# A hybrid decoder layer on one core: the memory tokens' projection one column tile later

## The chip, the cores and the metric

The kernel runs on one core of one Trainium2 chip. The time is device time in microseconds (us) of one execution, the median of several; lower is better. The engines are PE (matrix products), ACT, DVE and POOL (elementwise work of different kinds) and SP, which here only issues transfers; POOL issues the gathers from the paged cache. Matrix operands lie in SBUF, products in PSUM.

## The reference

One layer of a decoder trunk runs for two groups that share the weights: a prompt of 2048 tokens and a sample group of 8 x 4 tokens. The core of it:

```
h = rms_norm(x, pre_g)
z = h @ w_in                                   # 1024 -> 11 x 512 columns
ca, cb, cg, pu, pg, q, k, v, sg, mq, mg = split(z)
y_c = conv_branch(ca, cb, ...)                 # gated causal convolution, width 31
y_p = pool_branch(pu, ...)                     # causal means of 2, 4, 8, 16 tokens
y_s = stick_breaking_attention(q, k, v)        # prompt: causal; sample: 8192 cached tokens each
mk, mv = split(rms_norm(mem, mem_g) @ w_mem_kv)  # 256 memory tokens, 2 x 512 columns
y_m = softmax_attention(mq, mk, mv)
mix = concat(y_c*silu(cg), y_p*silu(pg), y_s*silu(sg), y_m*silu(mg))
y = rms_norm(x + rms_norm(mix @ w_out, post_g), final_g)
```

The new keys and values, the last rows of the convolution and pooling inputs and the memory keys and values are outputs too.

## The kernel before

**Stages.** First the projection z, with the sample group's attention over its cache woven into it; then the prompt's attention (`sb_prompt`), with small leftovers of the sample group as side work; then the output product. What PE does is in the order in which the program is written. A scheduler places the instructions of the other engines and of the queues, within what the data allow.

**The projection.** Each operand is split into a high and a low half, and a product is three matmuls (high by high, high by low, low by high) for each of the 8 slices of 128 of the 1024 inputs, so 24 matmuls (`mm3`). The prompt goes in two parts of 1024 tokens; part 0 also holds the 32 sample rows. A column tile is 128 columns of `w_in`: (q, 0) is the first of q. Part 0 has 44 column tiles, each in three row tiles of 384, 384 and 288 rows, part 1 has 44 in two row tiles of 512. `GROUPS[part]` lists them in the order in which they are done; most groups hold one column tile, the first of part 0 holds (q, 0) and (q, 1) together, then come (q, 2), (q, 3), (k, 0) to (k, 3), (v, 0) to (v, 3) and the rest. `z_groups` runs groups: it opens each, multiplies row tile by row tile, empties the product (`z_evac`) and yields the cost of every half product.

**Weights.** `SEQ_W` is the order in which weight tiles are loaded by SP (`load_w`, tile wr, 512 KB) and split (`split_w`: ACT makes whi, POOL wlo). There are two pairs of whi and wlo and two raw tiles; `fill_w` refills them whenever a column tile is done. The eight column tiles of the memory tokens' weight (`"mem"`) are inserted into this list by a table of pairs (number, place).

**The start.** `x_first` loads, normalises and transposes the prompt's first 1024 rows while the first group runs on what is ready. Once 768 rows are done, `mem_norm` is added to the tasks; it does the same for the 256 memory tokens (tiles xtm, xpsm, mhi, mlo). `tasks.step()` gives every live task one step. Then `mem_tokens` is handed to `z_groups` as `between`: after each product of a row tile one memory product (mz, 24 matmuls of 256 columns) is made, eight in all, and `mem_rows` empties it (mzt), turns it back and stores it (mko, mvo, and for later use mkd, mvd).

**The sample group.** When the memory pool is closed, `main` runs all remaining groups. Each cost it yields adds to `due`; whenever `due` reaches 1, one step of the generator `sample` is taken. It gathers cached keys and values (kt, vt, by POOL), turns the keys on DVE (T), forms scores (sSA), weights and products with the values (sO), in 64 rounds of about four steps. The line numbers are those of the profile:

```
total = 39 * 1056 / 512 * 5.12 + 44 * 1024 / 512 * 5.12
rate = (4 * NPAGE + 8) / (SEND * total)        # NPAGE 64, SEND 0.97
```

When the generator ends, its pool is closed, and the loader of the prompt's attention is made on the same space (`sb_loader`); it issues the first block's loads at once: four of kT, four of Q, one of V. These and the stores of the projection's last results (gsd, gcd, mixd, and ydw for the convolution) go through SP's one queue in order. `sb_prompt` then works in blocks of 512 queries, (head pair, block): scores S, two sigmoids on ACT (gam, be), a scan on DVE (E), products on POOL, transposes (AT) and products with the values (av).

Of the kernel before, what the change touches and what calls it, by code (L numbers as in the profile page):

```python
# [86 lines left out]
def kernel(  # L87
# [66 lines left out]
    def z_tile(name):  # L154
        return zps.tile([P, 512], F32, tag="z", name=name)
# [80 lines left out]
    def mm3(ps, whi, wlo, xhi, xlo, c0, c1):  # L236

        n = ND * 3
        i = 0
        for d in range(ND):  # L240
            for w, x in ((whi, xhi), (whi, xlo), (wlo, xhi)):
                pe.matmul(ps[:, : c1 - c0], lhsT=w[:, d, :], rhs=x[:, d, c0:c1], start=i == 0, stop=i == n - 1)
                i += 1
                if i == n // 2:
                    yield
# [12 lines left out]
    def k4(name, shape, dt):  # L258
        return st.tile(shape, dt, tag="k4", name=name, bufs=K4)
# [62 lines left out]
    def x_stream(part, ahead, tile_):  # L322

        todo = [(xp[PART * part + P * t : PART * part + P * (t + 1), :], P, P * t, f"p{part}_{t}") for t in range(8)]
        ready = []
        gpre = None
        loaded = []

        def norm():
            n, xt = loaded.pop(0)  # L330
            ready.append(norm_rows(xt, todo[n][1], gpre, rs1[:, n : n + 1]))

        for i, (src, rows, col, nm) in enumerate(todo):
            while len(ready) + len(loaded) < min(len(todo), i + ahead):
                n = len(ready) + len(loaded)
                xt = tile_(f"xt{todo[n][3]}")
                sp.dma_start(xt[: todo[n][1]], todo[n][0])
                if gpre is None:
                    gpre = big(f"gpre{part}")[:, :D]
                    sp.dma_start(gpre, pre_g[0].partition_broadcast(P))  # L340
                loaded.append((n, xt))
            if i == 0:
                yield
                yield
                norm()
            if loaded:
                norm()
            while X["free"] < col + rows:
                yield
            for hf in range(2):  # L350
                split_rows(ready[i], rows, xhi, xlo, col, hf, nm)
                if hf:
                    X["done", part] = col + rows
                yield
# [24 lines left out]
    def mem_norm(mp, M):  # L379
        mg_bc = mp.tile([P, D], F32, name="mg_bc", bufs=1)  # L380
        sp.dma_start(mg_bc, mem_g[0].partition_broadcast(P))
        M["hi"] = mp.tile([P, ND, NMEM], F32R, name="mhi", bufs=1)
        M["lo"] = mp.tile([P, ND, NMEM], F32R, name="mlo", bufs=1)
        rows = []
        for t in range(2):
            xt = mp.tile([P, D], F32, tag="xt", name=f"xtm{t}", bufs=XB)
            sp.dma_start(xt, mem_prompt[0, P * t : P * (t + 1), :])
            rows.append(norm_rows(xt, P, mg_bc))
        yield
        yield  # L390
        for t in range(2):
            for hf in range(2):
                split_rows(rows[t], P, M["hi"], M["lo"], P * t, hf, f"m{t}")
                yield
# [260 lines left out]
    def z_open(part, kind, c):  # L655

        s = {}
        if kind == "ca":
            U = s["U"] = state["U"] = big(f"U{part}_{c}")
            pool.tensor_copy(U[:, 0:CH], uhist[:, c, :])  # L660
        elif kind == "pu":
            s["pf"] = big(f"pf{part}_{c}")
            pool.tensor_copy(s["pf"][:, 0:PH], phist[:, c, :])
        elif kind == "mg":
            state["g"] = big(f"g{kind}{part}_{c}")
        elif kind == "pg":
            s["plw"] = st.tile([P, P], F32, tag="plw", name=f"plw{part}_{c}", bufs=1)
            wq.dma_start(s["plw"], pool_w[0, c])
        elif kind == "mq":
            s["kv"] = mem_kv(c, part)  # L670
        return s
# [80 lines left out]
    def z_close(part, kind, c, s):  # L752
        if kind == "cb":
            U = state["U"]
            pool.tensor_copy(uhist[:, c, :], U[:, PART : PART + CH])
            tasks.add(conv_dw(c, U, part))
        elif kind == "pu":
            pool.tensor_copy(phist[:, c, :], s["pf"][:, PART : PART + PH])
            state["d"] = pool_group(c, s["pf"], part)

    MAIN = ("ca", "cb", "pu", "cg", "pg", "mg")
    GROUPS = {0: [[("q", 0), ("q", 1)]] + [[(k, c)] for k in ("q", "k", "v") for c in range(2 if k == "q" else 0, 4)],
              1: [[(k, c)] for k in ("k", "v", "q") for c in range(4)]}
# [3 lines left out]
        GROUPS[part] += ([] if part == 0 else [[("ca", 3)], [("cb", 3)]]) + [[("pu", 3)], [("mg", 3)], [("mq", 3), ("pg", 3)]]  # L767
        GROUPS[part] += ([[("ca", 3)], [("cb", 3)]] if part == 0 else []) + [[("cg", 3), ("sg", 3)]]
    SEQ_W = [(p_,) + it for p_ in range(2) for g in GROUPS[p_] for it in g]
    for i, at in ((0, 3), (1, 4), (2, 5), (3, 7), (4, 8), (5, 9), (6, 11), (7, 12)):  # L770
        SEQ_W.insert(at, (0, "mem", i))
    raw, wsplit = {}, {}

# [5 lines left out]
    def fill_w(n=2):  # L779

        while len(wsplit) < n and (raw or SEQ_W):
            if not raw:
                next_raw()
            it = next(iter(raw))
            wsplit[it] = split_w(raw.pop(it), "%d%s%d" % it)
        while n == 2 and len(raw) < WR and SEQ_W:
            next_raw()

    def z_groups(part, groups, between=None):

        for g in groups:
            last = part == 0 and g is GROUPS[0][-1]
            fill_w()
            if last:
                X["free"] = 0
                tasks.add(x_stream(1, XA, lambda n: k4(n, [P, D], F32)))
            opened = [z_open(part, kind, c) for kind, c in g]
            cols = COLS[part]
            for ti, (c0, c1) in enumerate(cols):
                for j, (kind, c) in enumerate(g):  # L800
                    while X["done", part] < c1:
                        yield 0.0
                    ps = z_tile(f"z{part}{kind}{c}_{ti}")
                    half = 2.56 * (c1 - c0) / 512
                    for _ in mm3(ps, *wsplit[(part, kind, c)], xhi, xlo, c0, c1):
                        yield half
                    z_evac(part, kind, c, ti, c0, c1, ps, opened[j])
                    if ti == len(cols) - 1:
                        z_close(part, kind, c, opened[j])
                        del wsplit[(part, kind, c)]  # L810
                        fill_w()
                    if last and j == 1:
                        X["free"] = c1
                    yield half
                    if between is not None:
                        next(between, None)
                        yield 0.0
# [962 lines left out]
    with tc.tile_pool(name="mem", bufs=2, side="right") as mp:  # L1780
        M = {}
        xst = x_first(lambda n: mp.tile([P, D], F32, tag="xt", name=n, bufs=XB))
        for _ in range(X0):
            next(xst)
        tasks.add(xst)
        for _ in z_groups(0, GROUPS[0][:1]):
            tasks.step()
            if X["done", 0] >= XM and not M:
                M["gen"] = mem_norm(mp, M)
                tasks.add(M["gen"])  # L1790
        for _ in M["gen"]:
            pass

        sp.dma_start(conv_sample[0][:, 0 : CH - TS, :], state_conv[0][:, TS:CH, :])
        sp.dma_start(pool_sample[0][:, 0 : PH - TS, :], state_pool[0][:, TS:PH, :])
        sp.dma_start(bias_bc, sb_bias[0].partition_broadcast(P))
        dve.tensor_scalar(out=nbias_bc, in0=bias_bc, scalar1=-1.0, scalar2=None, op0=ALU.mult)
        tasks.add(params_and_histories(mp))
        mem = mem_tokens(mp, M)
        for _ in z_groups(0, GROUPS[0][1:4], mem):  # L1800
            tasks.step()
        for _ in range(3):
            tasks.step()
# [9 lines left out]
    sample = sample_all()  # L1813

    def main():
        yield from z_groups(0, GROUPS[0][4:12])
        tasks.add(later_stats())
        yield from z_groups(0, GROUPS[0][12:14])
        tasks.add(sample_keys())
        yield from z_groups(0, GROUPS[0][14:])  # L1820
        tasks.add(state_rows(0))
        yield from z_groups(1, GROUPS[1][:-2])
        tasks.add(state_rows(1))
        yield from z_groups(1, GROUPS[1][-2:])
# [205 lines left out]
    for n, x in enumerate(parts):  # L2030
# [8 lines left out]
        prod, i, h = x  # L2039
# [55 lines left out]
```

## Time and profile before

| what | value |
|---|---|
| median of three runs | 2423.75 us (2419.15 to 2426.24) |
| the profiled execution: its time / its span | 2418.47 us / 2416.7 us |
| mean granted clock of PE | 0.982 |
| PE busy | 2285.6 us |
| DVE / POOL / ACT busy | 1718.3 / 1306.8 / 1117.5 us |
| moved by the transfer engines | 562.14 MB, mean 233 GB/s |

Rows of a time line give the start, the length, the engine, the line, the operation, output and inputs and the count; in brackets stands how long the engine was idle just before and what ended that. Numbers of buffers are left out of names in the trace. PEld is PE's loading of weights, which overlaps its products; SPq is SP's transfer queue, whose rows are issues and not the transfers themselves.

### The profile page before, as it was taken

To read this page: it belongs to the slowest core of one execution; us is meant where nothing else is said; L and a number is where in the kernel's file an instruction comes from. 1 tells how busy PE (TensorE), PEld (TensorE's weight loads), DVE (VectorE), ACT (ScalarE), POOL (GpSimd) and SP (SyncE) were. 2 spreads that over 40 slices of the span, in tenths; PEclk is the share of its full clock that TensorE was granted. 3 is DMA by queue.
4 is the path that set the end of the run, shared out by engine and by line. 5 is a ranking of instruction groups with operands and counts; after the bars stand their busy time and mean duration, and the time that the engine had idled before them with its cause. 6 is when DMAs were issued, how large, how long until landed. Compare 5 with 4: busy or idle time off the path is not lost. (4 is left out here: it accounts for less than half of the span.)

```text
span 2416.7 us, 42137 instructions
## 1 busy us (share of the span) xinstructions
PE 2285.6 (95%) x15962; PEld 1774.5 (73%) x15962; DVE 1718.3 (71%) x2410; ACT 1117.5 (46%) x1939; POOL 1306.8 (54%) x1333
## 2 busy tenths in 40 slices
PE   7999999999999999999999998899999998989897
PEld 6998978898888777777777776455555556768775
DVE  5333774959757664587877777879798846687998
ACT  5322343242442322124242434788989954443554
POOL 2554544556574555655556564667877755453430
PEclk9999999999999999999999999999999999999998
DMA  5789988887778899987887767834333227887764
GB/s 179 223 260 298 348 290 287 284 272 263 263 254 292 277 344 325 323 287 262 275 270 269 262 218 179 239 79 117 89 88 79 64 64 242 266 272 254 245 234 170
DMA packets 340437, 562.14 MB, mean 233 GB/s; under 512 B 28481, under 2 KB 212929, under 8 KB 323834
## 3 DMA queue, kind: packets, MB, share of 16 engines
q1 hardware_dynamic: 284858, 290.72, 39.2%
q0 software_dynamic: 55376, 268.72, 31.3%
q8 instruction: 126, 2.06, 0.3%
q14 instruction: 77, 0.63, 0.1%
HBM read 469.28 MB, written 90.68 MB: 232 GB/s over the span
## 5 line engine op out<-in xcount | busy, mean ns | idle before, releaser
L959 DVE STREAM_TRANSPOSE T<-kt 128x1024 f32<-128x1024 f32 x256 | 308.9, 1226 | 183.4 <-PE sSA L972 177.2
L926 POOL DMA_INDIRECT vt<-in_cache_v_dram,idv x256 | 251.6, 983 | 242.1 <-PE sO L1011 181.5
L617 DVE SCALAR_TENSOR_TENSOR cacc<-U,par,cacc 128x512 f32<-128x512 f32 x480 | 360.2, 750 | 11.8
L1311 POOL TENSOR_TENSOR be<-be,E 128x512 f32<-128x512 f32 (+2 forms) x320 | 303.8, 957 | 118.4 <-DVE E L1302 52.4
L1302 DVE TENSOR_TENSOR_SCAN E<-gam,cr,ZM 128x513 f32<-128x513 f32 x192 | 232.8, 1262 | 15.1 <-ACT gam L1287 14.2
L926 POOL DMA_INDIRECT kt<-in_cache_k_dram,idk x128 | 126.2, 986 | 201.9 <-DVE T L959 146.8
L1322 PEld LDWEIGHTS AT<-ident,be 128*128 128x128 f32 x1088 | 117.7, 142 | 127.6 <-ACT at L1328 45.4
L1287 ACT ACTIVATE gam<-S,nbias_bc 128x1024 f32<-128x1024 f32 (+1 forms) x160 | 172.6, 1079 | 50.8 <-ACT be L1289 18.9
L1915 PE MATMUL acc<-wohi,mh 128*128 128x512 f32 (+1 forms) x480 | 193.3, 403 | 0.6 <-ACT mh L1669 0.6
L1915 PE MATMUL acc<-wolo,mh 128*128 128x512 f32 (+1 forms) x480 | 189.6, 395 | 0.0
L1915 PE MATMUL acc<-wohi,ml 128*128 128x512 f32 x448 | 178.1, 398 | 11.6 <-DVE ml L1680 11.6
L1282 PE MATMUL S<-kT,Q 128*128 128x512 f32 (+1 forms) x640 | 177.9, 401 | 6.8 <-DMA Q<-qd 2.7
L1289 ACT ACTIVATE be<-S,bias_bc 128x1024 f32<-128x1024 f32 (+1 forms) x160 | 171.6, 1073 | 0.0
L1322 PE MATMUL AT<-ident,be 128*128 128x128 f32 x1088 | 158.1, 284 | 14.1 <-ACT at L1328 4.2
L1338 PE MATMUL av<-at,V 128*64 128x512 f32 (+3 forms) x640 | 153.0, 557 | 1.7 <-DVE sbo L1343 1.7
L972 PE MATMUL sSA<-T,W 128*32 128x128 f32 x4096 | 139.2, 277 | 6.4 <-DVE T L959 5.6
L972 PEld LDWEIGHTS sSA<-T,W 128*32 128x32 f32 x4096 | 104.7, 110 | 43.6 <-issue 35.3
L1680 DVE TENSOR_TENSOR ml<-mr,mh 128x512 fp32r<-128x512 f32 x108 | 98.1, 914 | 38.4 <-ACT mh L1669 38.2
L1282 PEld LDWEIGHTS S<-kT,Q 128*128 128x128 f32 x640 | 107.1, 195 | 23.0 <-ACT be L1289 3.5
L1011 PE MATMUL sO<-vt,saT 128*32 128x512 f32 x1024 | 122.4, 592 | 0.0
L1299 DVE TENSOR_TENSOR_SCAN E<-gam,ZM 128x128 f32<-128x128 f32 (+3 forms) x128 | 96.4, 802 | 30.1 <-ACT gam L1287 25.2
L1328 ACT COPY at<-AT 128x512 f32<-128x512 f32 x192 | 108.9, 655 | 14.4 <-PE AT L1322 14.4
(571 smaller groups left out, 6043.7 us busy)
## 6 DMA issues: line engine op xcount, KB each, us to landing
Q<-qd SPq DMA_DIRECT2D x64, 256.0 KB
mr<-mixd SPq DMA_DIRECT2D x32, 512.0 KB
mr<-mixd SPq DMA_DIRECT2D x48, 256.0 KB
wor<-in_w_out_dram SPq DMA_DIRECT2D x20, 512.0 KB
xtp<-in_x_prompt_dram SPq DMA_DIRECT2D x16, 512.0 KB
kT<-kd SPq DMA_DIRECT2D x64, 128.0 KB
wor<-in_w_out_dram SPq DMA_DIRECT2D x32, 256.0 KB
msd<-mr SPq DMA_DIRECT2D x32, 256.0 KB
```

What stands on the lines that cost most here:

```text
L617: dve.scalar_tensor_tensor(out=ps, in0=U[:, a + k : a + k + H], scalar=wd[:, k : k + 1], in1=ps, op0=ALU.mult, op1=ALU.add)
L926: pool.indirect_dma_start(out=dst, out_offset=None, in_=rows, in_offset=bass.IndirectOffsetOnAxis(ap=idx, axis=0))
L959: dve.transpose(T[:, 2 * hh : 2 * hh + 2].rearrange("p s j t -> p (s j t)"), kt[:, 2 * hh : 2 * hh + 2].rearrange("p s j d -> p (s j d)"))
L972: pe.matmul(sSs[n][32 * g : 32 * g + 32, P * ml : P * (ml + 1)], lhsT=W[:, jj, :], rhs=T[:, :, jj, :], start=i == 0, stop=i == 3, tile_pos ...
L1282: pe.matmul(S[:, j, :w], lhsT=Q[hh][:, x, P * (q2 + j) : P * (q2 + j + 1)], rhs=KT[hp, hh, kc][:, :w], start=x == 0, stop=x == 1)
L1287: act.activation(out=ga[:, :, 512 - w : 512], in_=S[:, :, :w], func=AF.Sigmoid, bias=nbias_bc[:, h : h + 1], scale=-1.0)
L1289: act.activation(out=be[:, :, :w], in_=S[:, :, :w], func=AF.Sigmoid, bias=bias_bc[:, h : h + 1])
L1302: dve.tensor_tensor_scan(out=E[:, j][:, ::-1], data0=ga[:, j][:, ::-1], data1=ZM[:, 0:1].to_broadcast([P, 513]), initial=carry[hh, q2][:, ...
L1311: pool.tensor_tensor(out=be[:, j, :m], in0=be[:, j, :m], in1=E[:, j, 513 - w : 513 - w + m], op=ALU.mult)
L1322: pe.transpose(ap_[:, P * qt : P * (qt + 1)], A[hp, qb, kc, hh, qt][:, P * r : P * (r + 1)], ident)
L1338: pe.matmul(av[64 * hh : 64 * hh + 64, c], lhsT=V[:, 4 * kc + r, 64 * hh : 64 * hh + 64], rhs=ats.pop((hp, qb, kc, r, hh))[:, c], start=dg ...
L1915: pe.matmul(o[:rows], lhsT=m[a][:, k, :rows], rhs=W[prod, 4 * h + k][w], start=not cont and h == k == n == 0, stop=h == 1 and k == 3 and n ...
```

## The change

Three things move by one group in part 0. The table puts the eight memory weights one place later into `SEQ_W`. The start now runs two groups, (q, 0) with (q, 1), and (q, 2), before the memory products are handed over. The memory products go between the row tiles of (q, 3), (k, 0) and (k, 1) instead of (q, 2), (q, 3) and (k, 0), and `main` begins with (k, 2) instead of (k, 1). The line with `total` is unchanged, and nothing else is.

```
-    for i, at in ((0, 3), (1, 4), (2, 5), (3, 7), (4, 8), (5, 9), (6, 11), (7, 12)):
+    for i, at in ((0, 4), (1, 5), (2, 6), (3, 8), (4, 9), (5, 10), (6, 12), (7, 13)):
         SEQ_W.insert(at, (0, "mem", i))
...
-        for _ in z_groups(0, GROUPS[0][:1]):
+        for _ in z_groups(0, GROUPS[0][:2]):
             tasks.step()
             if X["done", 0] >= XM and not M:
                 M["gen"] = mem_norm(mp, M)
...
         mem = mem_tokens(mp, M)
-        for _ in z_groups(0, GROUPS[0][1:4], mem):
+        for _ in z_groups(0, GROUPS[0][2:5], mem):
             tasks.step()
...
     def main():
-        yield from z_groups(0, GROUPS[0][4:12])
+        yield from z_groups(0, GROUPS[0][5:12])
         tasks.add(later_stats())
```

More of the change, by code (lines that the diff above doesn't have):

```diff
@@ L769 @@
     SEQ_W = [(p_,) + it for p_ in range(2) for g in GROUPS[p_] for it in g]
-    for i, at in ((0, 3), (1, 4), (2, 5), (3, 7), (4, 8), (5, 9), (6, 11), (7, 12)):
+    for i, at in ((0, 4), (1, 5), (2, 6), (3, 8), (4, 9), (5, 10), (6, 12), (7, 13)):
         SEQ_W.insert(at, (0, "mem", i))
@@ L1785 @@
         tasks.add(xst)
-        for _ in z_groups(0, GROUPS[0][:1]):
+        for _ in z_groups(0, GROUPS[0][:2]):
             tasks.step()
@@ L1799 @@
         mem = mem_tokens(mp, M)
-        for _ in z_groups(0, GROUPS[0][1:4], mem):
+        for _ in z_groups(0, GROUPS[0][2:5], mem):
             tasks.step()
@@ L1815, in main @@
     def main():
-        yield from z_groups(0, GROUPS[0][4:12])
+        yield from z_groups(0, GROUPS[0][5:12])
         tasks.add(later_stats())
```

## The prediction

> **What bounds the kernel now.** I read the page first, then busy time by stretches of 50 us, then the time lines of PE (the matmul engine) and of SP's transfer queue where PE idles. A row of a stretch shows its length, busy us and count of PE, its weight loads, DVE, ACT and POOL, then granted clock, transfer share and GB/s.
>
> ```profile
> span 2416.7 us, 42137 instructions
> PE 2285.6 (95%) x15962; PEld 1774.5 (73%) x15962; DVE 1718.3 (71%) x2410; ACT 1117.5 (46%) x1939; POOL 1306.8 (54%) x1333
> 50.00:100.00 50.00, 48.45 (x353) 47.09 (x353) 19.80 (x36) 16.32 (x29) 25.94 (x19) 1.00 0.59 184
> 100.00:150.00 50.00, 46.79 (x310) 45.17 (x310) 18.08 (x43) 14.17 (x28) 28.00 (x31) 0.97 0.79 242
> 350.00:400.00 50.00, 45.32 (x399) 40.78 (x398) 24.04 (x38) 25.37 (x46) 24.60 (x23) 0.93 0.74 253
> 1450.00:1500.00 50.00, 44.55 (x212) 33.98 (x211) 40.29 (x60) 23.13 (x37) 20.63 (x38) 0.98 0.63 170
> 1500.00:1550.00 50.00, 43.11 (x252) 25.59 (x251) 37.50 (x55) 34.80 (x43) 27.97 (x41) 0.85 0.90 264
> ```
>
> PE is busy 95% of the span, in an order that is written out by hand. An edit that only reorders is therefore paid, or earns, where PE idles. The memory products lie in the first two stretches: 4.8 us idle in 100 us, nothing large. The largest hole is at 1490 us, where the projection with the sample group's work woven in ends and prompt attention begins: 5.5 and 6.9 us idle, at a lower granted clock.
>
> ```profile
> 1472.76 1.96 PE L1011 MATMUL sO<-vt,saT 128*32 128x512 f32 x16
> 1490.28 0.40 PE L242 MATMUL z1sg<-xhi,wlo1sg 128*128 128x512 f32 x1
> 1492.15 1.65 PE L1282 MATMUL S<-kT,Q 128*128 128x256 f32 x8 [1.47 <-DVE sg1sg L714]
> 1499.71 2.90 PE L1282 MATMUL S<-kT,Q 128*128 128x256 f32 x8 [1.68 <-DMA Q<-qd]
> 1503.67 1.19 PE L1282 MATMUL S<-kT,Q 128*128 128x256 f32 x4 [1.05 <-DMA Q<-qd]
> 1513.79 0.64 PE L1165 MATMUL smS<-mkbT,qm 128*32 128x256 f32 x8 [2.08 <-DMA mkbT<-mkTd]
> ```
>
> In the brackets stands the idle time just before and what ended it: three times a transfer. The sample's last products (sO, 1472.76) are 17.5 us ahead of the projection's last (1490.28); that lead is what the change touches.
>
> **The change part by part.** *The memory products.* Eight products of 24 matmuls and their weights go from the groups q2, q3, k0 to q3, k0, k1. Nothing is added or removed. ACT, which makes the high halves of the weights (whi) and empties the products (zt, mzt), before:
>
> ```order
> L232 COPY whi0mem_605<-wr0mem_250 128x1024
> L688 ACTIVATE zt0q_2_597<-z0q_2_572 128x288
> L688 ACTIVATE zt0q_0_648<-z0q_0_614 128x384
> L232 COPY whi0mem_680<-wr0mem_570 128x1024
> L416 COPY mzt_685<-mz_654 128x256
> ```
>
> And in the changed kernel, from the same place on:
>
> ```order
> L232 COPY whi0q_605<-wr0q_250 128x1024
> L688 ACTIVATE zt0q_2_597<-z0q_2_572 128x288
> L688 ACTIVATE zt0q_0_635<-z0q_0_610 128x384
> L688 ACTIVATE zt0q_1_666<-z0q_1_641 128x384
> L232 COPY whi0mem_705<-wr0mem_570 128x1024
> ```
>
> q3's weights are split where the first memory weights were, and q2's tiles follow each other without a memory product (mz) between. SP and POOL shift alike: one weight load of 512 KB stands for another, and one low half for another. What that can cost is a weight that comes late. The tightest case of before is k0's weight, split only once q3 is done:
>
> ```profile
> 100.83 2.40 POOL L233 TENSOR_TENSOR wlo0k<-wr0k,whi0k 128x1024 fp32r<-128x1024 f32 x1 [0.93 <-ACT whi0k L232]
> 103.28 0.45 PE L242 MATMUL z0k<-xhi,wlo0k 128*128 128x384 f32 x1 [0.20 <-POOL wlo0k L233]
> ```
>
> That cost 0.2 us. The same step comes once more in the new order, from q2 to the first memory weight, with the 24 matmuls of q3's first tile to cover it. I take 0; the ends are the 1.7 us that the stretch from 100 idles beyond the one from 50, either way. The rows of the tokens themselves stay: PE, DVE and POOL's order is unchanged up to q1's last tile, with the transposes of the memory rows in it.
>
> *The sample group's start.* `main` begins one group later. Its steps are dealt out by `due`, at 264 / (0.97 x 862.4) = 0.3156 per unit of projection cost, and `total` still counts 39 column tiles in part 0 where `main` now has 38. The sample's generator needs 268 calls, which are due at 268 / 0.3156 = 849.2 units. `main` had 862.4 units, a lead of 13.2; now it has 851.8, a lead of 2.6, one half of the last product. So sO and all that hangs on it move from 17.5 us to 12 matmuls ahead of the projection's end. Through the rest of the projection the sample's work lies 10.6 units later against the same tiles; PE's sum is the same, the chance meetings are others. I cost that at 0 with wide ends (rivals).
>
> *The first loads of prompt attention.* They are issued when the sample ends, and go on SP's queue. Before, with the semaphores that each waits for:
>
> ```order
> L601 DMA mixd<-po_3_1_14477 128x4x128 [waits DMAHW4_49,DVE_49]
> L1238 DMA kT_0_0_14518<-kd 64x512 [waits DMAHW5_49,PE_49]
> L1239 DMA Q_0_0_14519<-qd 64x2x512 [waits DMASW5_49,DMASW7_49,DMASW3_49,DMAHW6_49,DMASW1_49,PE_49]
> L1238 DMA kT_0_0_14518<-kd 64x512 [waits DMAHW7_49]
> L1239 DMA Q_0_0_14519<-qd 64x2x512 [waits DMAHW0_49]
> ```
>
> And in the changed kernel:
>
> ```order
> L540 DMA mixd<-mo_3_512_14567 128x4x128 [waits DMAHW7_49,DVE_49]
> L624 DMA ydw<-acc_3_1_14646 128x512 [waits DMAHW0_49,Activation_49]
> L1238 DMA kT_0_0_14601<-kd 64x512 [waits DMAHW1_49,PE_49]
> L1239 DMA Q_0_0_14602<-qd 64x2x512 [waits DMASW5_49,DMASW7_49,DMASW3_49,DMAHW2_49,DMASW1_49,PE_49]
> L1238 DMA kT_0_0_14601<-kd 64x512 [waits DMAHW3_49]
> ```
>
> The nine loads of block (0,0) (kT, Q and V) have moved behind four stores, the last of them the end of the convolution, `ydw<-acc_3_1`. When these rows ran before:
>
> ```profile
> kT<-kd SPq DMA_DIRECT2D x12, 128.0 KB
> Q<-qd SPq DMA_DIRECT2D x12, 256.0 KB
> V<-vd SPq DMA_DIRECT2D x1, 1024.0 KB
> 1474.78 0.53 SPq L1238 DMA_DIRECT2D kT<-kd  x1
> 1480.05 0.54 SPq L1244 DMA_DIRECT2D V<-vd  x1
> 1480.68 4.57 SPq L716 DMA_DIRECT2D gsd<-sg1sg  x1
> 1490.30 0.32 SPq L624 DMA_DIRECT2D ydw<-acc  x1
> 1490.67 0.46 SPq L1238 DMA_DIRECT2D kT<-kd  x1
> 1492.49 0.53 SPq L1239 DMA_DIRECT2D Q<-qd  x1
> 1504.94 7.97 SPq L1158 DMA_DIRECT2D mkbT<-mkTd  x8
> 1479.00:1482.00 3.00, 3.00 (x15) 2.42 (x14) 2.93 (x5) 0.00 (x0) 0.00 (x0) 1.00 0.97 219
> 1482.00:1485.00 3.00, 3.00 (x15) 2.42 (x14) 2.89 (x4) 0.60 (x1) 0.00 (x0) 1.00 1.09 203
> 1485.00:1488.00 3.00, 3.00 (x15) 2.42 (x14) 2.86 (x5) 0.00 (x0) 0.00 (x0) 1.00 1.21 289
> 1488.00:1491.00 3.00, 2.68 (x12) 1.83 (x10) 1.58 (x3) 0.81 (x2) 0.49 (x2) 1.00 0.79 265
> 1491.00:1494.00 3.00, 1.65 (x8) 1.14 (x8) 0.69 (x1) 1.38 (x3) 1.43 (x7) 1.00 0.69 223
> 1494.00:1497.00 3.00, 0.90 (x5) 0.70 (x6) 2.19 (x4) 3.00 (x5) 1.15 (x3) 1.00 0.72 145
> 1500.00:1503.00 3.00, 2.61 (x8) 1.70 (x7) 2.40 (x4) 1.80 (x4) 2.39 (x5) 0.50 1.07 223
> ```
>
> They ran from 1474.78 under a PE that was full. Now they start at about 1490.6, and block (1,·)'s loads, on which the scores at 1499.71 and 1503.67 already wait, come behind them. By issue alone: nine issues are 5.8 us (1474.78 to 1480.6), less 1.8 that the queue stood anyway between kT and Q (1490.67 to 1492.49): 4.0 us, the low end. By volume: four times 128 KB and 256 KB and V's 1 MB are 2.62 MB; at the mean of the three stretches from 1479 (237 GB/s) 11.1 us, of which 2.4 fit into the unused transfer share of 1488 to 1497 (3 us times 0.21, 0.31, 0.28): 8.7 us. The high end is 5.8 + 4.6 = 10.4, if the store behind V stands as long again (row 1480.68). I take 8.0, near the volume, because the transfer share is full from 1500 on, and a little under it since three stores that ran behind these loads now go ahead of them. The cover, 16 us of projection, is gone; what is late next is block (1,·), then the mkbT loads of 1504.94 and the smS at 1513.79, which stands in PE's order and holds all behind it. Nothing later in the attention stage waits for a fixed time, so the delay stays to the end.
>
> The Trainium skill (DMA: Bandwidth & Descriptors, section Bandwidth) gives 341 GB/s for a 1 MB transfer; by that figure, an estimate, the volume would take 7.7 us and the term would be 5.3. The rows above, with runs of the same loads, show 203 to 289, and they decide.
>
> *The clock.* A PE that idles more here runs longer at the lower clock (0.50 at 1500). Price of such a stretch at the start, behind another stall:
>
> ```profile
> 35.08 0.33 PE L242 MATMUL z0q<-xlo,whi0q 128*128 128x384 f32 x1
> 36.83 0.34 PE L242 MATMUL z0q<-xhi,wlo0q 128*128 128x384 f32 x1
> 43.79 0.63 PE L216 MATMUL xpsm<-ident,xtm 128*128 128x128 f32 x4 [3.66 <-DVE xtm L208]
> 44.17 0.52 PE L242 MATMUL z0q<-xhi,whi0q 128*128 128x384 f32 x1
> 47.69 0.37 PE L242 MATMUL z0q<-xhi,wlo0q 128*128 128x384 f32 x1
> ```
>
> Eleven matmuls at 0.32 us instead of 0.175: 1.6 us. At 1490 part of it is paid already, so 1.0, between 0 and 1.6.
>
> Sum: 0 + 0 + 8.0 + 1.0 = +9.0 us. Against the profiled execution, 2418.47 us (the span and 1.8 us around it), 2427.5; that execution is 5.3 us under the median of the three runs, 2423.75, so I expect a median of about 2433.
>
> **Rivals.** *The loads stay hidden* (not slower). PE's first score waits for sg1sg until 1492.15 anyway, and ACT for each pair of sigmoids; if the nine loads land within some 3 us and (1,·) follows at the issue's pace with shorter landings, 2 of the 4.0 us are left: 2426. For it: four loads are enough for the first score. Against it: the two rows that wait for Q now. It decides if block (1,·) lands before about 1502.
>
> *The sample's new phase removes a stall* (faster). One mechanism: between 350 and 400 PE lost 4.7 us to one wait for pL, and the granted clock of 0.93 over 50 us up to another 3.5.
>
> ```profile
> PE ms L509 <- DVE pL L551: 4.7, 1, 4.7
> DVE pL L551 <- DMA mkTd<-mkbT: 5.4, 1, 5.4
> ```
>
> DVE itself waited for a store (mkTd) to free a buffer. With the sample's gathers 10 us later that store may land sooner: -8.2, and it beats the tail only if the tail costs under about 1 us or a second such stall goes; with a tail of +0.5, 2416. By itself it makes 2424.5.
>
> *The new phase adds such a stall* (slower still): +4 to +8, 2437 to 2441.
>
> **How the numbers follow.** 0.3%, about what a measurement of this kernel can tell from no change, is 7.3 us, so the border lies at 2431.0. The tail as costed: 0.50, of which 0.40 lies above the border (2431 to 2437) and 0.10 below. A stall on top: 0.18, slower. Loads hidden, or the tail paid back by a stall that goes: 0.22, within 0.3%. Stall gone and tail cheap: 0.10, faster. Slower 0.58, same 0.32, faster 0.10. The range, 2419 to 2442, runs from the tail's low end with the memory stretch and a small realignment in favour up to an added stall.
>
> **What would show it.** In the changed kernel's profile: sO within 3 us of the projection's end; SP's ydw ahead of nine kT, Q and V issues; the first scores 3 to 5 us behind the projection's end instead of 1.5, waiting for kT or Q; the scores of (1,·) about 8 us later against that end; 57 to 130 us with no new wait. I am wrong if the attention stage starts as promptly as before, or if PE's idle time between 150 and 1450 moves by more than the tail.

## The result, and the profile after

The changed kernel takes 2437.11 us (median, 2432.59 to 2439.68); the kernel before, in six runs, 2419.59 us. The ratio is 1.0065, with a 95% interval of 1.0051 to 1.0078: 17.5 us by the medians, and slower by more than the measurement's 0.3%. The profiled execution of the changed kernel has a span of 2436.5 us, that of before 2416.7.

Busy time by stretches shows first where this came from. The first fence is the kernel before, the second the changed one; the columns are those of the prediction, and the last line of each is the sum.

```profile
60.00:430.00 370.00, 356.54 (x2994) 326.70 (x2993) 189.41 (x286) 124.91 (x245) 183.04 (x170) 0.98 0.84 283
430.00:800.00 370.00, 363.41 (x3254) 321.44 (x3254) 278.79 (x392) 130.43 (x250) 210.99 (x195) 1.00 0.80 273
800.00:860.00 60.00, 56.50 (x413) 42.66 (x412) 29.64 (x38) 17.39 (x31) 33.04 (x36) 0.94 0.86 299
860.00:1490.00 630.00, 627.54 (x4734) 469.40 (x4733) 449.66 (x583) 192.60 (x343) 349.87 (x310) 1.00 0.81 274
sum 1430.00, PE 1404.00 PEld 1160.20 DVE 947.50 ACT 465.33 POOL 776.94; mean PE 351.00 PEld 290.05 DVE 236.87 ACT 116.33 POOL 194.24
```

```profile
60.00:430.00 370.00, 355.57 (x2945) 327.11 (x2947) 185.94 (x285) 127.88 (x247) 181.43 (x168) 0.98 0.81 274
430.00:800.00 370.00, 356.05 (x3188) 316.53 (x3180) 256.32 (x367) 126.43 (x244) 204.53 (x190) 0.99 0.77 263
800.00:860.00 60.00, 53.48 (x393) 39.73 (x386) 40.84 (x54) 17.27 (x31) 28.63 (x32) 0.91 0.77 271
860.00:1490.00 630.00, 629.54 (x4830) 470.86 (x4829) 447.07 (x577) 198.07 (x351) 363.18 (x323) 1.00 0.82 281
sum 1430.00, PE 1394.64 PEld 1154.23 DVE 930.17 ACT 469.65 POOL 777.77; mean PE 348.66 PEld 288.56 DVE 232.54 ACT 117.41 POOL 194.44
```

In the 1430 us of the projection PE is busy 9.4 us less than before, 7.4 of them between 430 and 800 us, and the granted clock is a little lower where PE idles (1.00 to 0.99, 0.94 to 0.91). Nothing in the forecast's sum stands for this. The second place is the end of the projection. These are the changed kernel's two stretches, its time line of PE, and the time line of SP's queue:

```profile
1450.00:1500.00 50.00, 50.00 (x334) 37.93 (x338) 39.56 (x59) 22.41 (x41) 23.54 (x33) 1.00 0.44 144
1500.00:1550.00 50.00, 31.48 (x174) 17.80 (x167) 27.99 (x41) 22.96 (x27) 20.99 (x33) 0.76 0.96 262
```

```profile
1499.21 1.95 PE L1011 MATMUL sO<-vt,saT 128*32 128x512 f32 x16
1503.74 0.40 PE L242 MATMUL z1sg<-xhi,wlo1sg 128*128 128x512 f32 x1
1509.88 2.90 PE L1282 MATMUL S<-kT,Q 128*128 128x256 f32 x8 [5.74 <-DMA Q<-qd]
1521.66 2.90 PE L1282 MATMUL S<-kT,Q 128*128 128x256 f32 x8 [4.56 <-DMA Q<-qd]
1535.83 1.08 PE L1165 MATMUL smS<-mkbT,qm 128*32 128x256 f32 x8 [3.60 <-DMA mkbT<-mkTd]
```

```profile
1502.46 0.32 SPq L624 DMA_DIRECT2D ydw<-acc  x1
1502.87 0.53 SPq L1238 DMA_DIRECT2D kT<-kd  x1
1508.13 0.54 SPq L1244 DMA_DIRECT2D V<-vd  x1
1508.77 4.14 SPq L716 DMA_DIRECT2D gsd<-sg1sg  x1
1512.96 0.46 SPq L1238 DMA_DIRECT2D kT<-kd  x1
```

The projection's last matmul has moved from 1490.28 to 1503.74, by 13.5 us. The last sO stands 4.5 us ahead of it instead of 17.5. The loads of the first attention block are issued from 1502.87, behind ydw; the first score waits 5.74 us for them, 6.1 us behind the projection's last matmul instead of 1.9, and the scores of block (1,·) wait another 4.56 us. The smS, which stood 23.5 us behind that matmul, now stands 32.1 behind: 8.6 us. So there are two prices: 13.5 us before the end of the projection and 8.6 behind it (2.2 of them are not to be found at the end of the span any more; see what stays open).

What made the first price? The changed kernel's waits of PE between 60 and 1490 us (in total, times, longest):

```profile
PE ms L509 <- DVE pL L551: 6.3, 1, 6.3
PE z0pg L242 <- POOL wlo0pg L233: 5.1, 1, 5.1
PE z0sg L242 <- POOL wlo0sg L233: 2.7, 2, 2.4
PE py L596 <- ACT mkbT L443: 2.3, 1, 2.3
PE z0pu L242 <- POOL wlo0pu L233: 1.3, 1, 1.3
```

The wait for pL, 4.7 us before, did not go but grew to 6.3. The wait for the low half of a pg weight, wlo0pg, was 0.7 us in total before. POOL's time line says why it is 5.1 now; first before, then after (the rows named vt and kt are gathers):

```profile
667.41 0.95 POOL L926 DMA_INDIRECT vt<-in_cache_v_dram,idv  x1 [5.94 <-PE sO L1011]
...
672.47 0.95 POOL L926 DMA_INDIRECT kt<-in_cache_k_dram,idk  x1 [0.31 <-issue]
...
687.34 2.39 POOL L233 TENSOR_TENSOR wlo0pg<-wr0pg,whi0pg 128x1024 fp32r<-128x1024 f32 x1
...
690.58 0.99 POOL L926 DMA_INDIRECT vt<-in_cache_v_dram,idv  x1 [0.16 <-issue]
```

```profile
692.46 0.97 POOL L926 DMA_INDIRECT vt<-in_cache_v_dram,idv  x1 [0.15 <-issue]
...
697.47 0.94 POOL L926 DMA_INDIRECT kt<-in_cache_k_dram,idk  x1 [0.30 <-issue]
698.42 0.21 POOL L712 COPY gms<-gmg 128x32 f32<-128x32 f32 x1
698.59 2.33 POOL L233 TENSOR_TENSOR wlo0pg<-wr0pg,whi0pg 128x1024 fp32r<-128x1024 f32 x1
```

Counted from the sample group's start, the five gathers ahead of the low half in the changed kernel (one every 1.25 us) are numbers 149 to 153 of 384. In the kernel before the same five ran from 667.41 to 673.42 and were done 14 us ahead of the low half; those behind it, from 690.58 on, are of the next round. So the sample group's lag has put a round of gathers directly ahead of an operation that PE wants at once. The inputs of the low half were not what was late: ACT had made whi0pg out of wr0pg by 692.35, but POOL, whose operations run one after another, makes the low half at 698.59, and PE stands. The changed kernel's time line of PE at that place:

```profile
695.58 0.34 PE L242 MATMUL z0pg<-xlo,whi0pg 128*128 128x384 f32 x1
700.98 0.69 PE L242 MATMUL z0pg<-xhi,wlo0pg 128*128 128x384 f32 x1 [5.06 <-POOL wlo0pg L233]
701.47 0.52 PE L242 MATMUL z0pg<-xhi,whi0pg 128*128 128x384 f32 x1
...
704.03 0.52 PE L242 MATMUL z0pg<-xhi,wlo0pg 128*128 128x384 f32 x1
704.35 1.48 PE L509 MATMUL ms<-mkT,mh0mq 128*128 128x256 f32 x6
```

A pause costs more than its length: the ten matmuls from 700.98 to 704.35 take 3.37 us, one per 0.34 us, where they go at one per 0.175 us before the pause. That is another 1.6 us. The granted clock (third column from the right) stood at half in this stretch:

```profile
700.00:705.00 5.00, 4.02 (x14) 4.02 (x15) 0.00 (x0) 0.00 (x0) 0.93 (x1) 0.50 1.01 407
```

### The profile page after: what moved, and what is told of

Read it like the earlier page. It is cut to its first block, busy times and chain, and to the rows that moved or that the text cites. A ratio compares the mean times of both kernels' runs of the same rounds, so it can differ in the third digit from the quotient of the medians.

```text
span 2436.5 us, 42150 instructions
## 1 busy us (share of the span) xinstructions
PE 2290.8 (94%) x15962; PEld 1779.3 (73%) x15962; DVE 1713.4 (70%) x2410; ACT 1122.4 (46%) x1943; POOL 1309.3 (54%) x1333
## 5 line engine op out<-in xcount | busy, mean ns | idle before, releaser
L1302 DVE TENSOR_TENSOR_SCAN E<-gam,cr,ZM 128x513 f32<-128x513 f32 x192 | 232.8, 1262 | 15.1 <-ACT gam L1287 13.8
L1282 PE MATMUL S<-kT,Q 128*128 128x512 f32 (+1 forms) x640 | 178.0, 402 | 12.5 <-DMA Q<-qd 11.2
L972 PEld LDWEIGHTS sSA<-T,W 128*32 128x32 f32 x4096 | 104.5, 110 | 37.5 <-issue 32.4
```

What stands on the lines that cost most here:

```text
L972: pe.matmul(sSs[n][32 * g : 32 * g + 32, P * ml : P * (ml + 1)], lhsT=W[:, jj, :], rhs=T[:, :, jj, :], start=i == 0, stop=i == 3, tile_pos ...
L1282: pe.matmul(S[:, j, :w], lhsT=Q[hh][:, x, P * (q2 + j) : P * (q2 + j + 1)], rhs=KT[hp, hh, kc][:, :w], start=x == 0, stop=x == 1)
L1302: dve.tensor_tensor_scan(out=E[:, j][:, ::-1], data0=ga[:, j][:, ::-1], data1=ZM[:, 0:1].to_broadcast([P, 513]), initial=carry[hh, q2][:, ...
```

## The experiments

The theory after the first look (A): the change is slower because the sample group's steps, and POOL's gathers among them, lie one column tile later against the projection (the +13.5), and because its end comes so late that the attention's first loads are in the open (the +8). The rival (B): the later memory products make the loss in the projection. The table gives all runs. "Idle" is the sum of PE's idle times in the brackets of its time line from 60 us to the projection's last matmul; "end" is the start of that matmul; the last two columns are how far behind it the first score and smS start. The us columns are from the profiled execution of each, the ratio from repeated runs beside the kernel before (whose median lay between 2419.0 and 2420.9 us beside them).

| kernel | median us | ratio to before [95%] | idle | end | first score | smS |
|---|---|---|---|---|---|---|
| before | 2419.59 | | 25.5 | 1490.3 | +1.9 | +23.5 |
| after | 2437.11 | 1.0065 [1.0051, 1.0078] | 35.2 | 1503.7 | +6.1 | +32.1 |
| e1: before, sample 3.3 steps later | 2437.44 | 1.0075 [1.0056, 1.0095] | 38.3 | 1505.0 | +5.9 | +31.7 |
| e2: after, sample 3.3 steps earlier | 2425.93 | 1.0024 [1.0007, 1.0040] | 32.8 | 1498.1 | +1.9 | +24.9 |
| e3: before, loads' call later | 2417.08 | 0.9999 [0.9985, 1.0012] | 27.6 | 1491.7 | +1.9 | +23.0 |
| e4: after, total of 38 tiles | 2426.68 | 1.0025 [1.0015, 1.0034] | 32.4 | 1501.0 | +1.9 | +23.3 |
| e5: before, last step late | 2427.41 | 1.0024 [1.0010, 1.0038] | 26.3 | 1492.0 | +10.9 | +34.0 |
| e6: after, three low halves on DVE | 2420.08 | 0.9999 [0.9985, 1.0013] | 24.2 | 1488.6 | +6.2 | +32.1 |
| e7: before, one step later | 2430.57 | 1.0042 [1.0029, 1.0056] | 33.0 | 1501.9 | +1.8 | +25.4 |
| e8: before, one step earlier | 2438.94 | 1.0065 [1.0039, 1.0091] | 41.8 | 1515.0 | +1.8 | +24.3 |
| e9: e6 with the end dealt faster | 2420.51 | 1.0004 [0.9992, 1.0016] | 28.2 | 1495.2 | +1.9 | +23.5 |
| e10: after with the end dealt faster | 2431.48 | 1.0052 [1.0035, 1.0069] | 36.1 | 1506.6 | +1.9 | +24.5 |
| e11: before, three low halves on DVE | 2417.63 | 0.9984 [0.9973, 0.9995] | 29.4 | 1497.9 | +1.9 | +23.7 |
| e12: after, lag made up evenly | 2414.26 | 0.9979 [0.9966, 0.9993] | 25.5 | 1489.8 | +1.9 | +24.3 |

**e1: the sample group's lag alone**, put into the kernel before:

```
-    due, blk = 0.0, {}
+    due, blk = -10.56 * rate, {}
```

> The kernel before, with the sample group's steps dealt out 10.56 cost units later (due starts at -10.56 x rate) and the memory products left where they were. Theory A, the sample group's later start is the whole change: as slow as the changed kernel, +14 to +21 us over before, with the loads of attention's block (0,0) behind the convolution's last store. Rival B, the move of the memory products and their weights is what costs: within 4 us of before in the projection and only the tail's 8 us, so +5 to +10.

Measured: 2437.44 us against the changed kernel's 2437.11. The end of the projection, the waits (5.1 for wlo0pg, 1.3 for wlo0pu, 6.7 for pL) and the late first score are all there, with the memory products where they were. A holds; B is not needed for the loss.

**e2: the lag taken back**, in the changed kernel, by three steps at once at the start:

```
-    due, blk = 0.0, {}
+    due, blk = 10.56 * rate, {}
```

> The changed kernel, with the sample group's steps dealt out 10.56 cost units earlier (due starts at +10.56 x rate), so that they meet the same tiles as in the kernel before; the memory products stay moved. Theory A: back at the time of before, within 4 us. Rival B: still +8 us or more over before.

Measured: 11.2 us of the 17.5 are gone, the tail among them (smS at +24.9). 6.5 us stay. PE's idle time is 7.3 us above that of before, and most of it lies at the start: the three steps come at once at about 140 us, and PE then waits for the sample's page table, a wait that neither kernel has.

```profile
PE bps L878 <- DMA ptb<-in_page_table_dram: 6.1, 1, 6.1
```

**e3: the first loads alone later**, in the kernel before: the call that issues them waits 10.56 units.

```
-    sbr = bx = None
+    sbr = bx = left = None
...
                 sample = None
+                left = 10.56
+                break
+        if left is not None:
+            left -= cost
+            if left <= 0:
+                left = None
```

> The kernel before, with the sample group untouched and only the first loads of prompt attention (block (0,0)) issued where the changed kernel issues them, half a product before the projection's end. The tail as costed: +8 us (4 to 10.4) over before, the projection's end unmoved. Rival, loads hidden: under +3.

Measured: 2417.08 us, no slower; it did not do what it was made for. The nine loads stand ahead of the last ydw as before: the four of kT and of Q are issued from 1476.23 to 1483.5, and only V comes later, at 1487.77 instead of 1480.05 (first score at +1.9). So a later call in the program did not move these loads behind ydw in SP's row; by what rule the scheduler places them is not shown. It says nothing on the price of loads that come as late as in the changed kernel. The sample's last step itself has to come later, which is e5.

**e4: the total counted anew**, so that the lag shrinks along the way and is gone at the end:

```
-    total = 39 * 1056 / 512 * 5.12 + 44 * 1024 / 512 * 5.12
+    total = 38 * 1056 / 512 * 5.12 + 44 * 1024 / 512 * 5.12
```

> The changed kernel, with the total counted for 38 column tiles, so that the sample group ends 13 cost units ahead of the projection again. Tail as costed: 7 to 9 us of the loss go in the attention stage's start, so +6 to +12 over before if the projection's loss of 13 us stays; the sample group's steps meet other tiles again, so the projection's part may change by 5 us either way. Rival, the lead at the end does not matter: as slow as the changed kernel.

Measured: +7.2 us over before, within the range expected. The tail's price is gone (smS at +23.3), the projection still ends 10.8 us later than before. The waits in it are others than those of the changed kernel (4.93 us at 317 for po, 2.45 for wlo0sg, 2.91 for gmg, 2.88 for saT).

**e5: the tail alone.** In the kernel before, only the last of the sample's steps is held back by one column tile.

```
+    calls, held = 0, 10.56
...
         while sample is not None and due >= 1.0:
+            if calls == 267 and held > 0:
+                held -= cost
+                break
+            calls += 1
             due -= 1.0
```

> The kernel before with only the sample group's very last step held back by 10.56 units of the projection's cost (one column tile); the 266 steps ahead of it stand where they stood. The last two sums (sO, 16 matmuls), the end of the sample group and the nine first loads of prompt attention then come late, with the last store of ydw ahead of the loads in SP's row, as in the changed kernel. Nothing else moves. Theory 'the tail is a price of its own, whatever happened earlier': the projection ends where it ended (1490.3, +-2), the first score comes 5 to 7 us behind it instead of 1.9, the first AT 21 to 24 us instead of 14.4; 2427 us (+7 to +9). Rival 'the loads are late in the changed kernel only because of the stalls of the projection, and would be hidden here': first score 1.5 to 2.5 us behind the end, 2418 to 2421.

Measured: +6.9 us by the medians (2.4 to 9.2 by the interval), with the projection's end within 2 us of before. The tail has a price of its own. In numbers it went past the expectation: here sO came just behind the projection's last matmul, the first score waited 8.62 us, and smS stood 34.0 us behind the end.

```profile
1492.30 1.95 PE L1011 MATMUL sO<-vt,saT 128*32 128x512 f32 x16
1502.88 2.90 PE L1282 MATMUL S<-kT,Q 128*128 128x256 f32 x8 [8.62 <-DMA Q<-qd]
```

**e6: three low halves off POOL**, in the changed kernel:

```
-        pool.tensor_tensor(out=lo, in0=raw, ...)
+        (dve if nm in ("0pg3", "0pu3", "0sg1") else pool).tensor_tensor(out=lo, in0=raw, ...)
```

> The changed kernel with three low halves of weights (the tiles wlo0pg, wlo0pu and wlo0sg of one column group each, for which TensorE waits 5.06, 1.30 and 2.38 us there) made on VectorE instead of GpSimd, where they stand behind gathers of the cache rows. Theory 'these waits are GpSimd's order, the later sample group put its gathers ahead of the low halves': the three waits go, TensorE's idle time between 60 and 1490 us falls from 35.2 by 5 to 8.7, 2428 to 2432. Rival 'something else is late there too (the weights' DMA, the high halves)': another wait of the same length takes their place, 2436 to 2439. Second rival: VectorE, which now does three more operations of about 1 us each, makes new waits elsewhere, 2437 to 2442.

Measured: 2420.08 us, 17.0 less than the changed kernel, where 5 to 9 had been expected. The time line of DVE shows the operation, and the sum from 60 to 1490 us shows PE back at the level of the kernel before (1404.00):

```profile
685.90 1.21 DVE L233 TENSOR_TENSOR wlo0pg<-wr0pg,whi0pg 128x1024 fp32r<-128x1024 f32 x1
```

```profile
sum 1430.00, PE 1404.76 PEld 1161.29 DVE 944.46 ACT 471.45 POOL 770.06; mean PE 351.19 PEld 290.32 DVE 236.12 ACT 117.86 POOL 192.51
```

The three waits are gone (5.1, 1.3 and, for wlo0sg, 2.7 to 0.5: 8.6 us), PE's idle time falls by 11.0 and the projection ends 15.1 us earlier. So the place of these low halves in POOL's row is the cause of the largest part of the projection's loss, and each microsecond of pause was worth more than one. That the time also equals that of before although the tail is still open (smS at +32.1) was not foreseen; the rest of the difference lies behind smS, where the executions scatter.

**e7 and e8: one step later and one step earlier**, in the kernel before (`due` starts at -1.0 and at 1.0).

> The kernel before with the sample group one step of its 268 later (the count starts at -1; the change has the effect of about -3.4). Theory 'the loss grows with the lateness, since the gathers move step by step behind the weights' low halves': a third of what the shift of 3.4 steps gave (2437.4), 2422 to 2427, with the tail still hidden or half hidden. Rival 'the projection is erratic in the phase, each position makes its own stalls': anything from 2414 to 2440, with stalls in other places than those of the changed kernel. Third: no difference until a threshold, 2418 to 2421.

> The kernel before with the sample group one step of its 268 earlier (the count starts at +1). Theory 'the loss grows with lateness': no loss, 2412 to 2420 (a gain where the order of before still has stalls of 4.7 and 3.2 us that lateness made). Rival 'erratic in the phase': 2414 to 2440, with new stalls. The tail stays hidden in both: first score 1.5 to 2.5 us behind the projection's end.

Measured: +10.1 us for one step later, and +18.4 for one step earlier. "The loss grows with lateness" falls, and the rival holds, that each position makes its own stalls: a step earlier is as bad as 3.3 later, with the tail still hidden (smS at +24.3). Its waits are others again; PE's waits of e8 and its sum, 15.9 us of PE's busy time less than before:

```profile
PE sSA L972 <- ACT saT L1001: 8.7, 4, 3.4
PE sSA L972 <- DVE T L959: 6.5, 5, 4.5
PE py L596 <- DVE po L598: 4.6, 1, 4.6
```

```profile
sum 1430.00, PE 1388.11 PEld 1147.07 DVE 929.78 ACT 462.10 POOL 775.54; mean PE 347.03 PEld 286.77 DVE 232.45 ACT 115.52 POOL 193.89
```

The kernel before sits at a place of the sample group with few meetings; each of the three shifts tried, in both directions, makes 7 to 16 us more of idle time.

**e9 and e10: the tail taken away**, in e6 and in the changed kernel, by dealing the sample 2.6% faster through the second part:

```
-    due, blk = 0.0, {}
+    due, blk, spent = 0.0, {}, 0.0
...
-        due += rate * cost
+        spent += cost
+        due += rate * cost * (1 + 10.56 / 400 if 420 < spent <= 820 else 1)
```

> The changed kernel with the three low halves on VectorE (as in the run before it, 2420.1) and the sample group dealt 2.6% faster between 420 and 820 of the projection's 862 units of cost, so that it ends one column tile earlier and the loads of prompt attention stand ahead of the last ydw store again. Theory 'two separate prices, GpSimd's order and the tail': first score 1.5 to 2.5 us behind the projection's end instead of 6.2, 2411 to 2414, that is faster than both kernels. Rival 'the faster dealing makes new stalls in the second part of the projection': idle time of TensorE there grows from the 0.5 us seen, 2417 to 2424.

> The changed kernel with that faster dealing alone; the low halves stay on GpSimd. Theory of two separate prices: the first part of the projection keeps its stalls (the wait of 5.06 us for wlo0pg among them), the tail's 7 to 8 us go, 2428 to 2431. Rival 'the tail's price is hidden behind the same stalls, or the other way round': 2434 or more, or 2424 or less.

Measured: e10 is 5.6 us under the changed kernel, a little less than the 7 to 8 expected, with the 5 us wait for wlo0pg still there and the first score 1.9 us behind the end: in the time line the tail goes and the stalls stay. How much time that gives is less sure, since the intervals of the two ratios (1.0035 to 1.0069 and 1.0051 to 1.0078) overlap. e9 gained nothing on e6 (2420.51 and 2420.08): smS came 8.6 us earlier against the projection's end, and the end 6.6 us later. That is the rival, since the idle time up to the end grew from 24.2 to 28.2, behind 860 us from 0.5 to 4.4.

**e11: is POOL too full in any case?** The same three low halves on DVE in the kernel before.

> The kernel before with the same three low halves made on VectorE. In its trace TensorE has no wait over 1.2 us for these three tiles. Theory 'the low halves cost the changed kernel time because the gathers had moved ahead of them': nothing to gain here, 2416 to 2421. Rival 'GpSimd is too full in either kernel, and taking any of its work away helps whatever the order': 2403 to 2412, as much as the changed kernel gained (17 us).

Measured: 2417.63 us, 3.2 less than before (the interval is 0.5 to 2.7 thousandths): not the 17 us of e6. It is the order on POOL that cost the changed kernel time, not POOL's load. In its profiled execution, 3.4 us over its median, the projection ends 7.6 us later than before. Of these, 4.9 stand already at the first product of v (174.72 against 169.81), where the instructions are still the same; that product lies anywhere from 169.8 to 174.7 in before, e3, e5 and e11, so one execution's "end" is good to some 5 us.

**e12: the changed kernel with the lag made up evenly** over ten column tiles:

```
-    due, blk = 0.0, {}
+    due, blk, spent = 0.0, {}, 0.0
...
-        due += rate * cost
+        spent += cost
+        due += rate * cost * (1.1 if spent <= 105.6 else 1)
```

> The changed kernel with the sample group dealt 10% faster over its first ten column tiles (105.6 units), so that its lag of one column tile is made up evenly and not in one burst of steps; from the eleventh column tile on, GpSimd's gathers and low halves stand in the same order as in the kernel before, and the loads of prompt attention ahead of the last ydw store. What is left of the change is the later memory products and the first ten tiles' mixture. Theory 'the change costs only by the sample group's place against the projection and by the tail': 2417 to 2424, the projection ends 1488 to 1496, and the waits of before (about 2 us for wlo0sg near 341, about 3 us for T near 752) are there again while those of 5.06 us for wlo0pg and 1.30 us for wlo0pu are gone. Rival 'the later memory products cost something themselves' (as the +6 of the variant with the burst may have been): 2425 to 2431, the six microseconds being there before 260 us.

Measured: 2414.26 us, ratio 0.9979 [0.9966, 0.9993], so faster than both kernels, by 0.2% against before, which is less than the 0.3% that the forecast took as its border. PE's sum and waits are those of before:

```profile
sum 1430.00, PE 1404.11 PEld 1159.13 DVE 952.23 ACT 465.72 POOL 774.80; mean PE 351.03 PEld 289.78 DVE 238.06 ACT 116.43 POOL 193.70
```

```profile
PE sSA L972 <- DVE T L959: 5.9, 4, 4.0
PE ms L509 <- DVE pL L551: 4.3, 1, 4.3
PE z0sg L242 <- POOL wlo0sg L233: 2.0, 1, 2.0
PE z0pg L242 <- POOL wlo0pg L233: 0.7, 1, 0.7
```

The later memory products cost nothing by themselves, which leaves the burst as the cause of e2's +6.5. The time lies 3 us under the range expected; its profiled execution, with 2418.15 us one of its slowest, shows a projection as long as before, so what those 4.8 us are is open.

## Why the prediction was right or wrong

The direction was right and the time inside the range (2437.1 of 2419 to 2442), but the likeliest case, the tail alone, gives less than half of the loss. What happened is that case with the rival "the new phase adds such a stall" on top, which had given 2437 to 2441 and a chance of 0.18. That the time fell into that band is in part luck. The rival's stall was one like the wait for pL, at 4 to 8 us; what came were mainly waits for low halves on POOL, and 13.5 us. The sum stood on a median of before that was 4.2 us too high, and the 2.2 us behind smS came off again.

*The memory products, 0: right.* The stretches 50 to 150 us of the changed kernel hold 1.6 us less idle time than before (PE busy 96.8 against 95.2), e1 gives the same time without this part of the change, and e12 is no slower with it. As forecast, 57 to 130 us has no new wait of any size (1.2 us idle in all, 3.8 before).

*The sample group's start, "I cost that at 0 with wide ends": the step that failed.* It measured +13.5 us at the end of the projection: 9.7 of idle time, and about 3.3 of lower clock behind the pauses (an estimate: PE's busy time times what the granted clock lacks of 1.00, summed over stretches of 1 us from 60 us to the projection's end, is 8.8 us before and 12.1 after). The ends, +4 to +8 on one side, were too small too. The step took the meetings for chance without looking at one: POOL's row holds the low halves of the weights (2.4 us each, wanted by PE soon) among gathers that mostly come in groups of five or six (five take 6.3 us), and a shift of 3.3 steps can put a group directly ahead of a low half, as POOL's order in the changed kernel could have shown. The rival in the other direction, that the wait for pL would go, was wrong: it grew from 4.7 to 6.3 us. e7 and e8 say how far 0 was from a fair middle: all three shifts tried made the projection longer, by 11.6 to 24.7 us at its end.

*The first loads, +8.0: right in the time lines, less sure in the medians.* Over the kernels of the table whose first score comes 1.8 or 1.9 us behind the projection, smS starts 23.0 to 25.4 us behind the projection's last matmul, 24.0 in the mean of ten; in after, e1 and e6 it starts at 32.0 in the mean: 8.0 us, in which the lower clock there is contained. In e5, with sO itself behind the end, it starts at 34.0. By medians it is 6.9 (e5, 2.4 to 9.2 by the interval) and 5.6 (e10, where faster dealing costs idle time too). The condition of its high end came true (the store behind V stood 4.14 us again). Of its signs, sO came 4.5 us ahead of the projection's end, not within 3, and the first score came 6.1 us behind it, not 3 to 5. The scores of block (1,·) came 8.5 us later against that end, with 8 forecast. The transfers ran at the rate that the volume was costed at, 223 to 266 GB/s in these stretches of the changed kernel:

```profile
1505.00:1510.00 5.00, 0.12 (x1) 0.15 (x1) 0.50 (x1) 0.00 (x0) 0.89 (x5) 0.79 0.99 223
1515.00:1520.00 5.00, 2.08 (x4) 1.16 (x4) 1.99 (x4) 2.52 (x4) 2.96 (x4) 0.50 1.10 266
```

The figure of the Trainium skill (DMA: Bandwidth & Descriptors, section Bandwidth), by which the term would have been 5.3, is under the 8.0 us of the time lines; the medians, with their intervals, do not rule it out.

*The clock, +1.0:* it was costed at the attention's start alone, where no run shows it apart: smS moved by 8.6 us with loads and clock together, a little under the sum of 9.0. Behind the projection's new pauses no term stood for it, and there it came to the 3.3 us above. The price that its row showed, 1.6 us behind a pause, is what the pause at 700.98 cost again.

*The median:* the sum was set on 2423.75, and the kernel before, run more often, has 2419.6. That put the forecast 4.2 us up, and hid a part of the missing term: +9 was forecast and +17.5 measured.

By its own last sentence the prediction was wrong on one count: PE's idle time between 150 and 1450 us moved by more than the tail's 8 us (by 12.0, from 20.7 to 32.7).

*What stays open.* Behind smS the executions take between 894 and 903 us, with no order that follows the changes; the 2.2 us that the changed kernel seems to get back there lie within that, and so does the rest of e6's gain. Why e6, with its tail open, is no slower than before, and e9, with the tail closed, no faster than e6, is explained only that far. Why e12 is a little faster than before is not settled. Whether another place of the sample group is better still was not searched for.

## What to carry to other kernels

When an edit shifts one stream of work against another on engines whose order is fixed when the program is built, don't cost the new meetings at zero because the sums are equal: read the order on the side engines for what now stands ahead of an operation that the busy engine wants at once, and where the old place came out well, expect a shift to lose, as each of the three here did. If such an edit is wanted for another reason, give the shifted stream back its old place, evenly and not in one burst, as in e12. Loads that are issued when a helper stream ends are hidden only by what is left of the main stream, so look at that lead first.

## What the runs showed of the hardware

A pause of PE costs more than itself. Behind the pause of 5.06 us at 700.98 the granted clock was 0.50, and the matmuls came at half their rate for some 3.4 us. The Trainium skill (TensorE: Matmul & The Clock Gate, Part 1) says that the clock falls to half after an idle window of about 3.4 us and is back after about 3.4 us of work; the pause at 700.98 agrees. Short pauses close together went with the same. In the changed kernel PE pauses for 0.84, 1.48 and 2.38 us ahead of 812.4, 814.6 and 817.6, none of them as long as 3.4 us, and stands at half clock from 816 to 824:

```profile
812.00:816.00 4.00, 1.36 (x8) 0.84 (x8) 3.89 (x7) 0.59 (x1) 2.35 (x2) 0.87 0.88 312
816.00:820.00 4.00, 1.97 (x8) 1.57 (x8) 4.00 (x6) 1.54 (x3) 2.50 (x9) 0.50 0.81 275
820.00:824.00 4.00, 2.67 (x12) 1.72 (x12) 3.48 (x5) 1.37 (x3) 0.98 (x1) 0.50 0.93 253
```

Summed over the projection, the time at half clock (twice what the granted clock lacks of 1.00, in stretches of 1 us) is 20.5 us before and 34.1 in the changed kernel, and in all fourteen kernels of the table it is, within 0.1 us, a whole number of pieces of 3.41 us (from 3 pieces in e3 to 13 in e8). Over the kernels whose projection ended over 4 us later than before, its end moved by 1.1 to 2.0 us for each microsecond of idle time added; with the clock's share, estimated as above, the two add up to the move of the end within 1.5 us.

A gather of cache rows holds POOL for about 0.95 us, with 0.30 more until the next begins, so five of them delay POOL's arithmetic by 6.3 us; the same low half that takes POOL 2.33 us took DVE 1.21.
